# Moving the loop over overfull experts into the first expert pair, with a longer run of weight loads ahead of it

## The chip, the cores and the metric

The kernel runs on one core of one Trainium2 chip. The metric is the device time of one launch in microseconds; lower is better. The five instruction streams are TensorE (PE in the profile, with its weight loads shown as PEld), VectorE (DVE), ScalarE (ACT), GpSimd (POOL) and SyncE (SP). SP issues nearly all the weight transfers; the core's 16 DMA engines carry them out. All data are float32.

## The reference, cut to what matters

Three transformer layers run one after the other on 256 tokens of width 1024. Each layer first computes a modulation vector (silu of a condition vector times a weight matrix), then a mixer (attention, or in the third layer a mixture of attention, an MLP over chunks and a gated recurrence), and then a mixture of experts. The change touches the last part, which in the first two layers is:

```python
def grouped_moe(h, router_w, router_bias, w_gate, w_up, w_down):
    scores = sigmoid(t @ router_w)                 # 16 experts in 4 groups
    ...                                            # best group, then the best 2 of its 4 experts
    for e in range(N_EXPERTS):
        he = silu(t @ w_gate[e]) * (t @ w_up[e])   # 1024 -> 512
        out = out + gates[:, e:e + 1] * (he @ w_down[e])
```

The third layer has 32 experts and another router. An expert's three matrices are 2 MB each, so all experts together are 96, 96 and 192 MB, and every byte is read once.

## The kernel before, in words

**Experts in pairs.** `moe` handles two experts at a time, each with room for `CAP` = 64 tokens, so that the two fill 128 rows. `gather` (L1569) collects the tokens of eight experts with one-hot matrices. Then `body` runs for each pair: gate and up products (L1650), silu (L1655) and product (L1657), a transpose (L1666, copied on ACT in L1668), the down product (L1679), a weighting (`weigh`, L1684 to L1686), and one pair later `scatter` (L1714) back to the tokens, added to `x` (L1719). `back` (L1579) prepares the scatter matrix of a pair.

**Weight loads.** A pair needs 12 tiles of 1 MB (`load`, L1609): four each for gate, up and down. They live in the pool `u`, which has 17 such buffers, and SP issues them in program order. The loads are asked for by the letter `u` in an order string (each `u` is one step of the generator `ahead`), and at the head of each pair for those not yet asked for. Two more buffers of the pool hold the normalized tokens (`xs`) throughout the experts.

**The order strings.** `MIX_ORDER[0]`, `MIX_ORDER[1]` and `W2_ORDER` list, a letter at a time, the steps of the mixer of layers 0, 1 and 2 and the preparation of the experts: `M` the router's logits (two steps), `E` `ranks` (which expert and which place for each token, its products in L1527 to L1531), `F` the one-hot matrix of the first eight experts, `U` a broadcast of a modulation row (L443), `O` the gates, `L` a half of the gather, `l` `back`, `u` a load, `A` and `f` one modulation tile (`ada_tile`, two loads of 1 MB in L224 and eight products in L413), `9` a step of the third layer's context, interleaved into the second layer. A scheduler then orders each engine's instructions; SP's loads come out in the order of the strings, while the products of PE can move past one another unless `keep_in_program_order` pins them.

**The loop.** An expert may draw more than 64 tokens. `overflow` covers that with a hardware loop over such experts (L1728 reads their number `ni` into a register of each engine, L1729 is the loop). With this input the number is zero in all three layers; no line of the loop's body has an instruction in the trace. All five engines still meet at the loop's head and jump over its body. In the order strings the loop is the letter `!`, behind 12, 10 and 14 loads in layers 0, 1 and 2. What the program lists behind the loop can't be issued ahead of it, on any engine, SP among them. Once the strings are played, layer 0 and 1 close the next layer's modulation (`ada_close`: a copy of the sum, an add in L420 and 64 small products in L428), and `body` begins.

```python
        def ahead():
            for e0, n in ((0, 12), (2, 6)):
                for i in range(n):
                    load(e0, i)
                    yield
```

Of the kernel before, what the change touches and what calls it, by code (L numbers as in the profile page):

```python
# [11 lines left out]
F32R = mybir.dt.float32r  # L12
# [30 lines left out]
def _pack(inp):  # L43
# [68 lines left out]
    for l in range(3):  # L112
        bi = np.zeros((32, 512), np.float32)
        bi[:12] = (g("ada_b")[l] if l < 2 else g("b_mod_2")[0]).reshape(12, 512)
        if l == 2:
# [4 lines left out]

RAW = 2

W2_ORDER = "8f8GGKGKfKQQGfVVfKQfAYZZfQYb5QaBmanN6abc6bndW5cp4dc2mp43nfd2J.mqP13pq7r0sq107rHssTHXRergMijkMEFuOLULluuuuuuuuuuuuu!"
MIX_ORDER = ("00kkfkqiqvtfvqr4vf421321Kxw3xuzwzfKfyQKQyfVnTVQRAn55667JV78A8o.WPYXWXZYZfNpNeafbMdDuMEUFOLAuu,LuuuluuuuAu!uu",
             "0A0kkkqqqtvfvviffrKA12324341fKQxfKwxfyyQzzfQAIwTVR557667VJ.XV88oPYWWXYZ9Z9peabMdDUM9EFOLuLluuuuuuuuu!uuuu")
PRIME = 2

ENG = {
# [17 lines left out]
NB4 = 0  # L146

GE = 8
BUFS = {"u": 17, "b4": 8, "b2": 8, "tiny": 14, "G": 1}


class Halves:
# [10 lines left out]
class Gen:  # L163
# [223 lines left out]
                self.z2 = z  # L387
        return {"l": l, "lo": lo, "hi": hi, "n": 0}

    def ada_tile(self, st, V=None):  # L390

        n = st["n"]
        i = st["lo"] + n
        st["n"] += 1
        w = self.wload(self.ada_src(st["l"], i))
        if n == 0:
            st["R"] = self.ps()
        if i == max(st["lo"], st["hi"] - 3):
            b = f"bi{st['l']}"
            st["bi"] = self.late("b2", b, b, 32, self.nc.scalar)(b)  # L400
        z = self.z if st["l"] < 2 else self.z2
        last = i == st["hi"] - 1
        if V and n and not last:
            acc = self.t("b2", [128, 512])
            V.tensor_scalar(acc, w[:, 0, :], z[:, 0, 11:12], None, op0=OP.mult)
            for k in range(1, KC):
                V.scalar_tensor_tensor(acc, w[:, k, :], z[:, k, 11:12], acc, op0=OP.mult, op1=OP.add)
            self.nc.tensor.matmul(st["R"][0:32, :], self.unit[:, 11 - i:43 - i], acc, start=False, stop=False,
                                  skip_group_check=True)
            return  # L410
        for k in range(KC):
            j = k % 4
            self.nc.tensor.matmul(st["R"][32 * j:32 * j + 32, :], z[:, k, 11 - i:43 - i], w[:, k, :],  # L413
                                  start=(n == 0 and k < 4), stop=(last and k >= 4), skip_group_check=True)

    def ada_close(self, st):
        nc, l = self.nc, st["l"]
# [1065 lines left out]
    def moe(self, l, stG, side):  # L1483

        nc, tc, a = self.nc, self.tc, self.a
        V, A, G = nc.vector, nc.scalar, nc.gpsimd
        E = 16 if l < 2 else 32
# [5 lines left out]
        B_ = self.mod[l][:, 3]  # L1493
# [28 lines left out]
        def ranks():  # L1522

            mask = st["mask"] = self.t("tiny", [128, NT, E])
            st["rest"] = (self.route_a if l < 2 else self.route_b)(st["lg"], gates, mask)
            pr = st["pr"] = self.ps()
            nc.tensor.matmul(pr[:, 0:E], self.c("ut"), mask[:, 0], start=True, stop=True)  # L1527
            nc.tensor.matmul(pr[:, E:2 * E], self.c("ut"), mask[:, 1], start=True, stop=False)
            nc.tensor.matmul(pr[:, E:2 * E], self.ones, mask[:, 0], start=False, stop=True)
            for t in range(NT):  # L1530
                nc.tensor.matmul(pr[:, 128:128 + E], self.ones, mask[:, t], start=(t == 0), stop=(t == 1))  # L1531
            mf = mask.rearrange("p t e -> p (t e)")
            V.scalar_tensor_tensor(rk.rearrange("p t e -> p (t e)"), pr[:, :NT * E], -BIGR, mf, op0=OP.add, op1=OP.mult)
# [76 lines left out]
                W[(e0, *key)] = q  # L1610

        def ahead():
            for e0, n in ((0, 12), (2, 6)):
                for i in range(n):
                    load(e0, i)
                    yield

        def gathers():
            st["hs"] = rows_of()
# [6 lines left out]
        acts = {".": lambda: st.update(rw=self.late("b2", rn, rn)(rn)), "U": lambda: st.update(g2=self.bcast(stG(), 5, "G")), "E": ranks, "F": first, "O": gate_parts,  # L1626
                "l": lambda: st.update(nxt=back(st["Pt"], 0))}

        acts["!"] = lambda: self.overflow(l, E, st["xs"], A_, B_, gates, st["mask"], rk, ov, ni, st["g2"], wg, wu, wd)

        def body():
            g2, nxt = st["g2"], st["nxt"]
            hs, P = st["hs"], st["Pt"]
            pend = []
            for pr_ in range(E // 2):
                e0 = 2 * pr_
                for i in range(12):
                    load(e0, i)
                PT, gs = nxt
                more = pr_ + 1 < E // 2  # L1640
                turn = more and (e0 + 2) % GE == 0
                if turn:
                    P = places(e0 + 2)
                c0 = e0 % GE * CAP
                pgu = []
                for nm in "gu":
                    p = self.ps()
                    for k in range(KC):
                        for s in range(2):
                            nc.tensor.matmul(p[s * 64:(s + 1) * 64, :], hs[k // 2][:, k % 2, c0 + s * 64:c0 + (s + 1) * 64],  # L1650
                                             W[e0, nm, k // 4, s][:, k % 4, :], start=(k == 0), stop=(k == KC - 1), skip_group_check=True)
                    pgu.append(p)
                    if nm == "g":
                        sg = self.t("b2", [128, 512])
                        A.activation(sg, p, AF.Silu)  # L1655
                he = self.t("b2", [128, 512])
                V.tensor_mul(he, sg, pgu[1])  # L1657

                if pend:
                    self.scatter(pend, range(2))  # L1660
                if turn:
                    hs = rows_of()
                    gather(P, hs, 0)
                ph = self.ps()
                for k in range(4):
                    nc.tensor.transpose(ph[:, k * 128:(k + 1) * 128], he[:, k:512:4], self.ident)  # L1666
                heT = self.t("b2", [128, 4, 128])
                A.copy(heT, ph.rearrange("p (k c) -> p k c", k=4))  # L1668
                if turn:
                    gather(P, hs, 1)  # L1670
                if more:
                    nxt = back(P, e0 + 2)
                po = [self.ps() for _ in range(2)]
                oh, ol = (self.t("b4", [128, 2, 512], F32R) for _ in range(2))
                pend = [(PT, (oh, ol))]

                def down(n, k, w):
                    for s in range(2):
                        nc.tensor.matmul(po[n][s * 64:(s + 1) * 64, :], heT[:, k, s * 64:(s + 1) * 64], w(s),  # L1679
                                         start=(k == 0), stop=(k == 3), skip_group_check=True)  # L1680

                def weigh(n):
                    o = self.t("b2", [128, 512])
                    V.scalar_tensor_tensor(o, po[n], gs, g2[:, n * 512:(n + 1) * 512], op0=OP.mult, op1=OP.mult)  # L1684
                    A.copy(oh[:, n], o)  # L1685
                    (G if more else V).tensor_tensor(ol[:, n], o, oh[:, n].bitcast(F32), op=OP.subtract)  # L1686

                if more:
                    for h in range(2):
                        for n in range(2):  # L1690
                            for k in range(2 * h, 2 * h + 2):
                                down(n, k, lambda s: W[e0, "d", h, s][:, k % 2, n * 512:(n + 1) * 512])
                    next(side, None)
                    for n in range(2):
                        weigh(n)
                else:
                    for n in range(2):
                        for k in range(4):
                            down(n, k, lambda s: W[e0, "d", n, s][:, k])
                        weigh(n)  # L1700
                    for n in range(2):
                        self.scatter(pend, (n,), l == max(self.layers))
# [89 lines left out]
    def run(self):  # L1792
# [7 lines left out]
            st[key] = self.ada_open(l, lo, hi)  # L1800
            q[c].extend([st[key]] * (hi - lo))

        def fill(c, V=None):
            if q[c]:
                self.ada_tile(q[c].pop(0), V)

        def done(key):

# [10 lines left out]
        def layer(l, nxt):  # L1819
            self.l = l  # L1820
            ada(l, 4, 10, f"B{l}")
            ada(l, 10, 12, f"G{l}")
            if nxt:
                ada(l + 1, 0, 4, f"A{l + 1}", "A")
            steps, acts, body = self.moe(l, lambda: done(f"G{l}"), side)
            steps["9"] = side
            acts["f"] = lambda: fill("f")
            acts[","] = lambda: fill("f", self.nc.vector)
            if nxt:
                acts["A"] = lambda: fill("A")  # L1830
                acts["C"] = lambda: done(f"A{l + 1}")
            stB = lambda: done(f"B{l}")
            if l < 2:
                self.mix(l, stB, (steps, acts))
            else:
                self.mix2(stB, (steps, acts))
            if nxt:
                done(f"A{l + 1}")
            body()
# [52 lines left out]
```

## Time and profile before

| | |
|---|---|
| median of 3 runs | 1563.3 us (1558.73 to 1563.33) |
| the profiled execution | 1559.93 us, of which the span is 1558.1 us |
| moved by DMA | 540.85 MB, mean 347 GB/s |
| busy: PE / DVE / ACT / POOL | 1398.8 / 628.2 / 403.0 / 111.6 us |
| mean granted clock of TensorE | 0.966 of full speed |

The profile divides the span into busy time of each engine, the share of time that the DMA engines were busy, and the waits of each engine by what ended them. A busy share is a mean over the span: layer 0's mixer ends near 200 us and its experts near 440, layer 1's experts run from 644 to 885, and layer 2's from 1094 to the end. In the transfers a share near 1.0 at about 420 GB/s is the most that any stretch shows. The two levels of TensorE's clock appear as 1.00 and 0.50.

### The profile page before, as it was taken

Reading aid. Unit: us, or ns where it says so; the run is one execution under the profiler, and the core shown is the slowest. Engines: PE = TensorE matmul, PEld = TensorE weight load, DVE = VectorE, ACT = ScalarE, POOL = GpSimd, SP = SyncE. Lnnn points to the kernel's source line nnn. Section 1 sums busy time; section 2 is a strip of 40 time slices with the busy share of each in tenths; the row PEclk is TensorE's granted clock in tenths of the full one; section 3 lists DMA queues with packets and bytes.
Section 4 is the critical chain, followed back from the end, with each engine's and each line's share of the span. In section 5 each row is a group of like instructions: output and inputs, shape, how many; then the busy total and the mean of one; then the engine's idle time right before and its main releaser. Section 6 shows DMA issues by size and latency. Waiting matters only on the chain. (4 is left out here: it accounts for less than half of the span.)

```text
span 1558.1 us, 18392 instructions
## 1 busy us (share of the span) xinstructions
PE 1398.8 (90%) x7074; PEld 738.3 (47%) x7074; DVE 628.2 (40%) x1441; ACT 403.0 (26%) x717; POOL 111.6 (7%) x96
## 2 busy tenths in 40 slices
PE   5999889998879989899999898697899989988987
PEld 2676543443346556434544375475235434334332
DVE  3777621221176675243212569865022212212122
ACT  2455311011053553232111365532101011101000
POOL 0000101101000000001001000101001010001000
PEclk9999979999999999999999999798999999999999
DMA  9987859999989947499999967147899999999997
GB/s 363 330 328 275 342 201 422 421 421 421 413 309 380 349 162 308 180 415 415 421 421 420 356 219 273 60 136 297 322 421 421 421 421 421 421 421 421 420 422 294
DMA packets 131071, 540.85 MB, mean 347 GB/s; under 512 B 8600, under 2 KB 13856, under 8 KB 83360
## 3 DMA queue, kind: packets, MB, share of 16 engines
q1 hardware_dynamic: 128032, 533.73, 86.4%
q10 hardware_dynamic: 2320, 3.89, 0.8%
q0 software_dynamic: 624, 1.98, 0.4%
q8 instruction: 59, 0.97, 0.2%
q14 instruction: 36, 0.29, 0.1%
HBM read 538.49 MB, written 1.06 MB: 346 GB/s over the span
## 5 line engine op out<-in xcount | busy, mean ns | idle before, releaser
L1650 PE MATMUL ps<-u,b 128*64 128x512 f32 x2048 | 471.8, 600 | 49.2 <-DMA u<-in_w_dram 32.0
L1650 PEld LDWEIGHTS ps<-u,b 128*64 128x64 f32 x2048 | 160.6, 138 | 348.7 <-issue 264.8
L265 PE MATMUL ps<-u 128*128 128x512 f32 x1104 | 279.1, 403 | 6.9 <-ACT u L517 5.5
L1679 PE MATMUL ps<-u,b 128*64 128x512 f32 x1024 | 233.9, 597 | 13.7 <-ACT b L1668 13.7
L265 PEld LDWEIGHTS ps<-u 128*128 128x128 f32 x1104 | 203.5, 190 | 79.6 <-issue 23.0
L1657 DVE TENSOR_TENSOR b<-b,ps 128x512 f32<-128x512 f32 x32 | 22.0, 688 | 483.4 <-PE ps L1650 467.7
L1679 PEld LDWEIGHTS ps<-u,b 128*64 128x64 f32 x1024 | 78.1, 136 | 143.7 <-issue 122.9
L1686 POOL TENSOR_TENSOR b<-b,b 128x512 fp32r<-128x512 f32 x58 | 78.0, 1356 | 800.4 <-ACT b L1685 699.7
L1684 DVE SCALAR_TENSOR_TENSOR b<-ps,tiny,G 128x512 f32<-128x512 f32 x64 | 48.0, 750 | 179.8 <-PE ps L1679 177.7
L196 DVE TENSOR_TENSOR u<-u 128x2048 fp32r<-128x2048 f32 (+1 forms) x48 | 105.4, 2208 | 4.8 <-ACT u L185 4.7
L413 PE MATMUL ps<-u,z 128*32 128x512 f32 x576 | 83.5, 638 | 16.3 <-DVE z L382 13.2
L1685 ACT CAST b<-b 128x512 fp32r<-128x512 f32 x64 | 39.4, 618 | 206.3 <-DVE b L1684 206.3
L185 ACT CAST u<-u 128x2048 fp32r<-128x2048 f32 x44 | 82.7, 1913 | 17.8 <-DMA u<-in_a_w_qkv_dram 15.2
L1668 ACT COPY b<-ps 128x512 f32<-128x512 f32 x32 | 18.7, 585 | 259.7 <-PE ps L1666 259.7
L1719 DVE TENSOR_TENSOR x<-x,ps 128x512 f32<-128x512 f32 x128 | 79.4, 679 | 1.8 <-PE ps L1714 1.8
L1569 PE MATMUL ps<-b,u 128*128 128x512 f32 x256 | 72.2, 438 | 3.1 <-DVE b L1555 3.1
L1655 ACT ACTIVATE b<-ps 128x512 f32<-128x512 f32 x32 | 19.1, 597 | 210.7 <-PE ps L1650 210.7
L1714 PE MATMUL ps<-b,b 128*128 128x512 f32 x256 | 69.4, 409 | 3.2 <-DVE b L1686 1.9
L1569 PEld LDWEIGHTS ps<-b,u 128*128 128x128 f32 x256 | 66.2, 330 | 7.9 <-DVE b L1555 3.3
L1714 PEld LDWEIGHTS ps<-b,b 128*128 128x128 f32 x256 | 45.3, 188 | 39.4 <-issue 26.0
L185 ACT COPY b<-ps 128x512 f32<-128x512 f32 (+1 forms) x61 | 32.5, 558 | 72.6 <-PE ps L265 34.8
L517 ACT ACTIVATE b<-ps,mod,mA 128x512 f32<-128x512 f32 x32 | 24.9, 780 | 100.5 <-PE ps L1569 100.5
(346 smaller groups left out, 1125.5 us busy)
## 6 DMA issues: line engine op xcount, KB each, us to landing
u<-in_w_dram SPq DMA_DIRECT2D x192, 1024.0 KB, 19.8
u<-in_moe_w_gate_dram SPq DMA_DIRECT2D x64, 1024.0 KB, 14.4
u<-in_moe_w_up_dram SPq DMA_DIRECT2D x64, 1024.0 KB, 16.2
u<-in_moe_w_down_dram SPq DMA_DIRECT2D x64, 1024.0 KB, 16.8
u<-in_ada_w_dram SPq DMA_DIRECT2D x48, 1024.0 KB, 10.1
u<-in_w_mod_dram SPq DMA_DIRECT2D x24, 1024.0 KB, 7.2
u<-in_w_in_dram SPq DMA_DIRECT2D x14, 1024.0 KB, 7.3
u<-in_a_w_qkv_dram SPq DMA_DIRECT2D x12, 1024.0 KB, 14.6
```

The source lines that it names most:

```text
L185: (e.copy if e is self.nc.scalar else e.tensor_copy)(out, in_)
L196: self.pick(site, options).tensor_tensor(out, a, b, op=op)
L265: self.nc.tensor.matmul(p, x[a][:, k, t * 128:(t + 1) * 128], w[b][:, k % 4], start=start and i == 0 and k == ks[0], stop=stop and i == 2 ...
L413: self.nc.tensor.matmul(st["R"][32 * j:32 * j + 32, :], z[:, k, 11 - i:43 - i], w[:, k, :], start=(n == 0 and k < 4), stop=(last and k >= ...
L1569: nc.tensor.matmul(p, q[:, t, k:D:KC], P[:, t], start=(t == 0 and i == 0), stop=(t == 1 and i == 1))
L1650: nc.tensor.matmul(p[s * 64:(s + 1) * 64, :], hs[k // 2][:, k % 2, c0 + s * 64:c0 + (s + 1) * 64], W[e0, nm, k // 4, s][:, k % 4, :], star ...
L1679: nc.tensor.matmul(po[n][s * 64:(s + 1) * 64, :], heT[:, k, s * 64:(s + 1) * 64], w(s), start=(k == 0), stop=(k == 3), skip_group_check=True)
L1684: V.scalar_tensor_tensor(o, po[n], gs, g2[:, n * 512:(n + 1) * 512], op0=OP.mult, op1=OP.mult)
L1685: A.copy(oh[:, n], o)
L1686: (G if more else V).tensor_tensor(ol[:, n], o, oh[:, n].bitcast(F32), op=OP.subtract)
L1714: ins = nc.tensor.matmul(p, PT[:, t * 128:(t + 1) * 128], o[:, n, :], start=(i == 0), stop=(i == len(ops) - 1))
L1719: nc.vector.tensor_add(xs, xs, p)
```

## The change

The letter `!` leaves the order strings. The loop is now called inside `body`, in the first pair, between its down products and its weighting. `ahead` no longer lists 18 loads but 12 + `SECOND[l]`, that is 28, 24 and 28 in the three layers; those that the strings don't ask for are asked for at the head of the first pair, before its products. The strings ask for 17, 13 and 17 (before: 14 in each, those behind `!` included). The pool `u` gets an 18th buffer, and `b4` and `b2` a ninth. In layer 0 the two modulation tiles of the next layer that stood behind the gather (letters `A`) become two letters `=` ahead of `E`: their 16 products and the first product of `ranks` are pinned in this order. The output buffers of a pair (`oh`, `ol`) are taken later.

```diff
-W2_ORDER = "...MEFuOLULluuuuuuuuuuuuu!"
-MIX_ORDER = ("...DuMEUFOLAuu,LuuuluuuuAu!uu",
-             "...DUM9EFOLuLluuuuuuuuu!uuuu")
+W2_ORDER = "...MEFuOLULluuuuuuuuuuuuuuuu"
+MIX_ORDER = ("...DuM==EUFOLuu,Luuuluuuuuuuuuu",
+             "...DUM9EFOLuLluuuuuuuuuuuu")
-BUFS = {"u": 17, "b4": 8, "b2": 8, "tiny": 14, "G": 1}
+SECOND = (16, 12, 16)
+BUFS = {"u": 18, "b4": 9, "b2": 9, "tiny": 14, "G": 1}
...
-            self.nc.tensor.matmul(st["R"][32 * j:32 * j + 32, :], z[:, k, 11 - i:43 - i], w[:, k, :],
-                                  start=(n == 0 and k < 4), stop=(last and k >= 4), skip_group_check=True)
+            ins = self.nc.tensor.matmul(st["R"][32 * j:32 * j + 32, :], z[:, k, 11 - i:43 - i], w[:, k, :],
+                                        start=(n == 0 and k < 4), stop=(last and k >= 4), skip_group_check=True)
+            if pin:
+                self.tc.keep_in_program_order(ins)
...
-            nc.tensor.matmul(pr[:, 0:E], self.c("ut"), mask[:, 0], start=True, stop=True)
+            ins = nc.tensor.matmul(pr[:, 0:E], self.c("ut"), mask[:, 0], start=True, stop=True)
+            if l == 0:
+                tc.keep_in_program_order(ins)
...
-            for e0, n in ((0, 12), (2, 6)):
-                for i in range(n):
-                    load(e0, i)
-                    yield
+            for i in range(12 + SECOND[l]):
+                load(i // 12 * 2, i % 12)
+                yield
...
-        acts["!"] = lambda: self.overflow(l, E, st["xs"], A_, B_, gates, st["mask"], rk, ov, ni, st["g2"], wg, wu, wd)
+        over = lambda: self.overflow(l, E, st["xs"], A_, B_, gates, st["mask"], rk, ov, ni, st["g2"], wg, wu, wd)
...
                 for i in range(12):
                     load(e0, i)
+                for i in range(0 if pr_ else SECOND[l]):
+                    load(2 + i // 12 * 2, i % 12)
...
-                oh, ol = (self.t("b4", [128, 2, 512], F32R) for _ in range(2))
-                pend = [(PT, (oh, ol))]
...
+                    if not pr_:
+                        over()
+                    pend = [places_out()]
                     next(side, None)
                     for n in range(2):
                         weigh(n)
...
+                acts["="] = lambda: fill("A", pin=True)
```

## Rows read from the trace of the kernel before

**Rows 1.** Stretches: busy us of the engines, granted clock, DMA share, GB/s.
```profile
230.00:440.00 210.00, 194.94 (x881) 82.76 (x878) 43.23 (x75) 24.28 (x43) 18.73 (x14) 1.00 1.02 418
650.00:885.00 235.00, 223.46 (x1002) 102.77 (x999) 67.05 (x154) 49.22 (x79) 19.79 (x17) 0.99 1.02 415
885.00:1080.00 195.00, 166.65 (x1173) 114.14 (x1172) 149.80 (x360) 91.05 (x153) 11.60 (x11) 0.92 0.59 212
```

**Rows 2.** The same view, narrow, around the three loops.
```profile
162.00:201.00 39.00, 31.22 (x183) 21.42 (x182) 22.45 (x77) 9.37 (x18) 7.39 (x4) 0.84 1.00 398
201.00:217.00 16.00, 15.08 (x62) 10.02 (x60) 5.57 (x15) 5.12 (x8) 0.00 (x0) 0.85 0.02 6
226.50:228.50 2.00, 2.00 (x12) 0.67 (x10) 0.00 (x0) 0.00 (x0) 0.00 (x0) 1.00 0.42 107
...
624.80:645.00 20.20, 15.86 (x62) 12.20 (x62) 10.25 (x34) 5.32 (x9) 1.60 (x1) 0.92 0.02 6
...
1079.50:1092.00 12.50, 10.00 (x34) 8.18 (x32) 4.39 (x14) 4.78 (x8) 0.00 (x0) 0.86 0.03 10
...
1096.00:1102.00 6.00, 6.00 (x20) 1.74 (x18) 0.00 (x0) 0.00 (x0) 0.00 (x0) 0.67 0.06 14
```

**Rows 3.** SP's load issues around the loops of layers 0, 1 and 2.
```profile
185.23 1.19 SPq L224 DMA_DIRECT2D u<-in_ada_w_dram  x2
...
216.77 2.76 SPq L1609 DMA_DIRECT2D u<-in_moe_w_gate_dram  x3
...
610.42 37.98 SPq L1609 DMA_DIRECT2D u<-in_moe_w_down_dram  x4
...
L1609 SPq DMA_DIRECT2D u<-in_w_dram x3: 332/335/432, 1091.7 to 1101.3; - x3
```

**Rows 4.** The loop's branches on PE: ns min, median, max, all three layers.
```profile
L1729 PEldq COMPARE_BRANCH  x9: 70/182/3269, 214.9 to 1094.4; - x9
```

**Rows 5.** PE in order of time: start, us, group, idle before it.
```profile
198.32 0.61 PE L1527 MATMUL ps<-tiny,cst 128*128 128x16 f32 x2 [5.02 <-DVE tiny L1429]
...
203.25 5.57 PE L1569 MATMUL ps<-b,u 128*128 128x512 f32 x16
208.74 1.06 PE L413 MATMUL ps<-u,z 128*32 128x512 f32 x8
...
214.16 1.92 PE L413 MATMUL ps<-u,z 128*32 128x512 f32 x16
218.84 2.11 PE L428 MATMUL ps<-cst,b 128*64 128x12 f32 x32 [2.75 <-DVE b L420]
220.78 11.43 PE L1650 MATMUL ps<-u,b 128*64 128x512 f32 x40
...
644.39 13.96 PE L1650 MATMUL ps<-u,b 128*64 128x512 f32 x64 [2.12 <-DVEq L1729]
...
1094.60 16.59 PE L1650 MATMUL ps<-u,b 128*64 128x512 f32 x64 [5.10 <-issue]
```

**Rows 6.** What PE waited for: layers 0, 1, 2 (us, times, longest).
```profile
PE ps L1650 <- DMA u<-in_moe_w_up_dram: 6.6, 5, 1.4
PE ps L1650 <- DMA u<-in_moe_w_gate_dram: 2.6, 2, 1.3
...
PE ps L1650 <- DVEq L1729: 2.1, 1, 2.1
...
PE ps L1650 <- DMA u<-in_w_dram: 32.0, 26, 1.4
```

**Rows 7.** The chain that ended last, in layer 2: start, us, what.
```profile
1120.59 13.73 PE ps L1650 x64
1134.32 2.05 PE ps L1714 x8
...
1137.51 7.09 PE ps L1679 x32
...
1516.28 19.83 DMA u<-in_w_dram
```

**Rows 8.** DMA issues by tile: count, KB each, median us to landing.
```profile
b<-in_pack_dram POOLq DMA_DIRECT2D x2, 64.0 KB, 5.1
```

More of the change, by code (lines that the diff above doesn't have):

```diff
@@ L121 @@
 RAW = 2
-W2_ORDER = "8f8GGKGKfKQQGfVVfKQfAYZZfQYb5QaBmanN6abc6bndW5cp4dc2mp43nfd2J.mqP13pq7r0sq107rHssTHXRergMijkMEFuOLULluuuuuuuuuuuuu!"
-MIX_ORDER = ("00kkfkqiqvtfvqr4vf421321Kxw3xuzwzfKfyQKQyfVnTVQRAn55667JV78A8o.WPYXWXZYZfNpNeafbMdDuMEUFOLAuu,LuuuluuuuAu!uu",
-             "0A0kkkqqqtvfvviffrKA12324341fKQxfKwxfyyQzzfQAIwTVR557667VJ.XV88oPYWWXYZ9Z9peabMdDUM9EFOLuLluuuuuuuuu!uuuu")
+W2_ORDER = "8f8GGKGKfKQQGfVVfKQfAYZZfQYb5QaBmanN6abc6bndW5cp4dc2mp43nfd2J.mqP13pq7r0sq107rHssTHXRergMijkMEFuOLULluuuuuuuuuuuuuuuu"
+MIX_ORDER = ("00kkfkqiqvtfvqr4vf421321Kxw3xuzwzfKfyQKQyfVnTVQRAn55667JV78A8o.WPYXWXZYZfNpNeafbMdDuM==EUFOLuu,Luuuluuuuuuuuuu",
+             "0A0kkkqqqtvfvviffrKA12324341fKQxfKwxfyyQzzfQAIwTVR557667VJ.XV88oPYWWXYZ9Z9peabMdDUM9EFOLuLluuuuuuuuuuuu")
 PRIME = 2
@@ L388, in ada_open, with ada_tile @@
         return {"l": l, "lo": lo, "hi": hi, "n": 0}
-    def ada_tile(self, st, V=None):
+    def ada_tile(self, st, V=None, pin=False):
         n = st["n"]
@@ L1680, in down, with places_out @@
                                          start=(k == 0), stop=(k == 3), skip_group_check=True)
+                def places_out():
+                    oh, ol = (self.t("b4", [128, 2, 512], F32R) for _ in range(2))
+                    return PT, (oh, ol)
                 def weigh(n):
+                    oh, ol = pend[0][1]
                     o = self.t("b2", [128, 512])
@@ L1696, in body @@
                 else:
+                    pend = [places_out()]
                     for n in range(2):
@@ L1801, in ada, with fill @@
             q[c].extend([st[key]] * (hi - lo))
-        def fill(c, V=None):
+        def fill(c, V=None, pin=False):
             if q[c]:
-                self.ada_tile(q[c].pop(0), V)
+                self.ada_tile(q[c].pop(0), V, pin)
         def done(key):
```

## The prediction

> **What bounds the kernel now.** I began with the stretches of the whole span [rows 1]. In the experts of layers 0 and 1 the transfers run at 415 to 418 GB/s with a DMA share of 1.02, so nothing more fits in; PE is busy for 93 and 95% there as well. In layer 2's mixer the share is 0.59, and its 28.3 us of idle PE are spread over short dependent steps. Next I asked which wait is last in each set of experts [rows 6]. In layer 0 PE waits for weights for 6.6 + 2.6 = 9.2 us in all, in layer 1 never (the row shown is its wait at the loop), in layer 2 for 32.0 us. So layer 2 is bound by transfers, layer 1 by PE, layer 0 by both within 9.2 us.
>
> Then the places where the transfers stand still, in narrow stretches [rows 2]. They rest at a share of 0.02 to 0.03 from 201 to 217, from 624.8 to 645 and from 1079.5 to 1092 us, each time at a loop. Two reasons meet there. SP sits at the head of the loop until the slowest engine has come, and behind it stand the next loads: it issues at 216.77, 644 and 1091.7 again [rows 3]. And the pool is nearly full: in layers 0 and 2 the transfers starve a second time after three loads and one (0.42 from 226.5 to 228.5, 0.06 from 1096 to 1102), until the first gate products give buffers back. In a set of experts bound by transfers such a hole is lost for good.
>
> **Prices.** One load is 1.05 MB at 418 GB/s, 2.5 us; a load lands 19.83 us after its issue [rows 7], so eight are in flight. A pair's gate and up products take 13.73 us, its down products 7.09, and 3.2 us lie between (1134.33 to 1137.51) [rows 7]. The first two buffers come free after a quarter of the 13.73 us, 3.4 us. From SP's issue to flowing data I count 1 us (issue at 1101.3, share near 1 from 1102) [rows 2, 3].
>
> **Layer 0: holes and start.** Before, 12 loads were done by 201 us, three followed at 216.77, and load 16 began at 228.5. After, 18 buffers less the two of the tokens hold 16 loads, provided that the modulation tiles have given theirs back. They have: pinned ahead of `ranks`, they fall into the 5.02 us for which PE waits for the routing anyway (ended at 198.32) [rows 5]. One and a half tiles are left for that gap, 1.06 + 1.92 = 3.0 us at full clock; at half clock 6.0, which would hold `ranks` up by 1 us. Their two loads per tile move forward on SP past pair 0's loads and are back in time: the last tile's were issued at 185.23 [rows 3] and now stand some eleven loads earlier. So the transfers go on for four loads, to 201 + 10 = 211 us.
>
> PE's order to pair 0 loses 1.06 us of a tile between the gathers, 1.92 us of one behind them, the loop's 2.75 us, and has 2.11 us of closing products that can go into a gap [rows 5]: `back` ended at 214.2, now near 213.1, and pair 0 starts between 213 and 216; I take 214.5 for 220.78, 6.3 us earlier. Load 17 flows at 214.5 + 3.4 + 1 = 218.9, which puts load 16 at 216.4 instead of 228.5: **12 us earlier** (10.6 to 13.6 by the start). Is PE fast enough? It gains 6.3 us, and 2.85 us because the first 40 products ran 11.43 us where 13.73 x 40 / 64 = 8.6 would do [rows 5, 7]; it loses the loop inside the pair (3 us, below). With its 9.2 us of waits that makes 15.4, so the 12 stand. With the dearest loop, a half-clock start and a start at 216 it makes 9.
>
> **The loop in its new place.** The register reads, the meeting and the jump are the same; the PE idle ahead of its next work was 2.75, 2.12 and 5.10 us [rows 5], the longest with a jump of 3.27 us [rows 4]. The trace shows no loop in mid-pair. Two things differ: ACT and DVE have nothing left that PE waits for, and SP comes after PE, since the last loads of the 28 (24) go out only as the down products free their buffers. I take 3 us, near the two shorter ones, and keep 2.1 to 5.1. After the 5.10 us the granted clock was 0.67 [rows 2] and the pair took 16.59 us for 13.73: 2.9 us more, which belongs to the dear end. Behind the loop now stand, on DVE, ACT and POOL, pair 0's weighting; who waits for it is the scatter, which comes after pair 1's 13.73 us, so nothing. On SP stand loads 29 and later. In layer 2, taking pair 0's start from the next paragraph, the down products end at 1089.5 + 13.7 + 3.2 + 7.1 = 1113.5; loads 17 to 28 flow from 1093.9 to 1123.9; the next buffers are free at 1113.5 + 3 + 3.4 and their loads flow at 1120.9: covered by 3 us. At the dear end (5.1 us, half clock) they flow at 1126.5, a hole of 2.6 us. Layer 0 has the same margin.
>
> **Layer 2.** 14 loads were done by 1079.5, one more followed, load 16 began at 1102. After: 16 loads without a pause to 1084.5; pair 0 starts where `back` ended, at 1094.60 - 5.10 = 1089.5; load 17 flows at 1089.5 + 3.4 + 1 = 1093.9, load 16 so to say at 1091.4: **10.6 us earlier**, 8 with the hole. PE follows, with 32 us of waits in hand.
>
> **Layer 1.** The same count would let the transfers resume about 5 us earlier, but PE never waits for them here, so this buys nothing. PE saves 2.1 us ahead of pair 0 and pays 3 behind its down products: **0.9 us slower**, between 2.1 faster (loop hidden altogether) and 5.9 slower (5.1 + 2.9 - 2.1).
>
> **Rest.** The ninth buffers of `b4` and `b2`, the later `oh` and `ol`, and the pins themselves issue nothing. They and the 18th buffer give the scheduler another order in the mixers, on either side; of the 28.3 us of idle PE in layer 2's mixer I allow a seventh, 4 us, each way.
>
> **Sum.** 12 - 0.9 + 10.6 = 21.7 us off the profiled execution's 1559.9: 1538. That execution lies 3.4 us under the median of the runs, so I forecast **1540 us**.
>
> **A rule that speaks against it.** In the rows, one jump of PE cost 3.27 us and the median of the nine 0.18 [rows 4]. The Trainium skill (Runtime: NRT & Kernel Launch, section "Instruction fetch mechanics") says that a taken branch whose target lies outside the two pages at hand makes the engine wait for a DMA fetch. By that rule every skip of a long loop body would pay, and the first rival below would hold; the trace bears it out for one loop in three.
>
> **Rivals.** *Dear loop:* all three loops stall PE for 5.1 us and the clock falls to its half each time. With a stall of S us (above 3) the gains become 14.6 - S in layer 0, -0.8 - S in layer 1 and 13.2 - S in layer 2, together 27 - 3S; at 5.1 that is 11.7, or 1548 us. *Slower:* the same mechanism, but the fetch queues behind the weights, which now run at full share while the loops before found the DMA idle (0.02 to 0.03) [rows 2]. The formula passes zero at S = 9 us and 0.3% slower at 10.6. If the fetch landed as late as a load does, 19.8 us, the sum is 32 us slower, 1592. Against it: 64 KB pieces on another queue land after 5.1 us [rows 8] while the loads' own queue takes 19.8. *The lead does not come:* some tile keeps two buffers through the gathers, 14 loads stand ready instead of 16, and the change moves little but the loop. Layers 0 and 2 lose two loads each, 5 us: 21.7 - 10 = 11.7, or 1548. The full pool of before (12 loads, 2 of the tokens and 3 loads more make 17 in layer 0) speaks against it. *The mixers:* the new order costs what the experts gain, 15 to 20 us, in stretches where PE has 0.59 of DMA share beside it [rows 1]: about 1560.
>
> **Chances.** The forecast, 1530 to 1547: 0.55. Dear loop: 0.15. No lead: 0.08. Mixers eat it: 0.08. Slower by the fetch: 0.09. Better than 1530 because the extra buffers help the mixers too: 0.05. What a measurement can tell from no change is about 0.3%, 4.7 us. Faster than that: 0.55 + 0.15 + 0.08 + 0.05, less 0.02 for tails, 0.81; within 0.3%: the mixers' 0.08 and a little of the tails, 0.09; slower: 0.10. The range 1530 to 1556 leaves out the slower case, most of the mixers' case and the best one, 0.2 in all.
>
> **What would show it.** Right: no hole in the transfers from 162 to 211 us, then one hole of 8 us (211 to 219) where there were two, and in layer 2 one of some 9 us where there were 12.5 and 6; load 16 near 216 in layer 0, near 1080 in layer 2 by its own clock (1091 less layer 0's 12, plus 1); PE's waits for weights in layer 0 down from 9.2 to about 3 us (15.4 - 12). Layer 1's experts as long as before within 2 us. At each loop, now between L1679 of pair 0 and L1650 of pair 1, 2 to 5 us of idle PE with a DMA share still near 1. Wrong: an idle PE of over 9 us there, a DMA share that falls behind the loop, `ranks` of layer 0 later than 199 us, or mixers that are longer than before.

## The result, and the profile after

The changed kernel takes **1577.45 us** (median of 4 runs, 1575.23 to 1578.81), the kernel before 1562.99 us beside it: a ratio of 1.0107, 95% interval 1.0092 to 1.0122. It is 1% slower, where 1540 us was forecast. The profiled execution took 1578.81 us, its span 1577.0, 18.9 us more than the span before.

What PE waited for answers to [rows 6]; the line of gate and up products is now L1659, the loop is L1745, the mixer's line that stands behind the loop in layer 1 is L529:

```profile
PE ps L1659 <- SPq L1745: 30.5, 2, 15.5
PE ps L1659 <- DMA u<-in_w_dram: 26.2, 22, 1.3
...
PE ps L529 <- SPq L1745: 14.5, 1, 14.5
...
PE ps L1659 <- DMA u<-in_moe_w_up_dram: 2.6, 2, 1.3
PE ps L1659 <- DMA u<-in_moe_w_gate_dram: 0.6, 1, 0.6
```

Waits for weights went down, in layer 0 from 9.2 to 3.2 us, as far as forecast. But PE now stands 45 us at the loop, 15 in each layer, and what releases it is SP. In order of time (start, us, group, idle before it), around the starts of [rows 5] and around the loop's new place:

```profile
191.36 5.72 PE L416 MATMUL ps<-u,z 128*32 128x512 f32 x32
198.33 0.40 PE L1532 MATMUL ps<-tiny,cst 128*128 128x16 f32 x2 [1.25 <-DVE tiny L1434]
...
213.89 16.70 PE L1659 MATMUL ps<-u,b 128*64 128x512 f32 x64
...
232.91 7.09 PE L1686 MATMUL ps<-u,b 128*64 128x512 f32 x32 [0.49 <-ACT b L1677]
254.91 7.67 PE L1659 MATMUL ps<-u,b 128*64 128x512 f32 x22 [14.92 <-SPq L1745]
...
661.29 7.14 PE L1686 MATMUL ps<-u,b 128*64 128x512 f32 x32 [0.49 <-ACT b L1677]
682.97 9.18 PE L529 MATMUL ps<-u 128*128 128x512 f32 x16 [14.54 <-SPq L1745]
...
1122.91 7.14 PE L1686 MATMUL ps<-u,b 128*64 128x512 f32 x32 [0.47 <-ACT b L1677]
1145.58 16.79 PE L1659 MATMUL ps<-u,b 128*64 128x512 f32 x64 [15.53 <-SPq L1745]
```

The down products of pair 0 (L1686) end at 240.0, 668.4 and 1130.1 us; then PE does nothing until 254.9, 683.0 and 1145.6. The stretches around the first two show what the transfers did meanwhile (us of PE, PEld, DVE, ACT and POOL, granted clock, DMA share, GB/s):

```profile
240.00:250.00 10.00, 0.00 (x0) 0.00 (x0) 0.00 (x0) 0.00 (x0) 0.00 (x0) 0.67 1.02 422
251.00:252.00 1.00, 0.00 (x0) 0.00 (x0) 0.00 (x0) 0.00 (x0) 0.00 (x0) 0.50 0.69 287
252.00:253.00 1.00, 0.00 (x0) 0.00 (x0) 0.00 (x0) 0.00 (x0) 0.00 (x0) 0.50 0.12 49
253.00:254.00 1.00, 0.00 (x0) 0.00 (x0) 0.00 (x0) 0.00 (x0) 0.00 (x0) 0.50 0.02 8
254.00:262.00 8.00, 7.09 (x22) 2.15 (x24) 1.41 (x2) 1.24 (x2) 2.49 (x2) 0.60 0.00 2
262.00:264.00 2.00, 2.00 (x12) 0.69 (x10) 0.00 (x0) 0.00 (x0) 0.00 (x0) 1.00 0.87 221
...
682.00:692.00 10.00, 9.03 (x16) 3.75 (x16) 1.41 (x2) 0.00 (x0) 0.00 (x0) 0.74 0.00 1
```

Read them from the top: the weights flow at full rate while PE and every other engine do nothing; at 252 us they run out; at 254.9 us PE starts again; and only then, in a pool full of weights, does PE free the buffers for the next loads, which flow at 262. One stall thus opened a hole of 10 us in the transfers. In the hole's first part the granted clock is 0.50 to 0.60, near or at the lower of TensorE's two levels (1.2 of 2.4 GHz), behind 15 us without a product. Layer 2's pair 1 (its row at 1145.58) took 16.79 us where a pair at the full clock takes 13.95.

That PE starts when the last load has landed is no coincidence. The loop's semaphore events step through the stall; in each row: engine, kind, count, ns, first and last start:

```profile
L1745 SPq EVENT_SEMAPHORE  x2: 17/17/17, 246.5 to 249.0; - x2
L1745 ACTq EVENT_SEMAPHORE  x2: 38/38/38, 246.5 to 249.0; - x2
L1745 PEldq EVENT_SEMAPHORE  x2: 51/51/51, 246.5 to 249.0; - x2
...
L1745 SPq EVENT_SEMAPHORE  x1: 17/17/17, 251.5 to 251.5; - x1
L1745 PEldq EVENT_SEMAPHORE  x1: 51/51/51, 251.5 to 251.5; - x1
...
L1745 SPq EVENT_SEMAPHORE  x5: 17/17/17, 253.9 to 254.2; - x5
L1745 PEldq EVENT_SEMAPHORE  x6: 51/51/51, 253.9 to 254.5; - x6
```

At 246.5, 249.0 and 251.5 the engines get past one semaphore each, at 253.9 past the rest, all at the same moments, 2.5 us apart: that is the 2.5 us of one load. The program itself names what they wait for. In its list of instructions, SP's way past the body of layer 0's loop is a wait for `SP_sequencer_49`, then one wait each for `DMAHW0_49` to `DMAHW7_49`, then an unconditional branch. These eight are the semaphores on which SP's loads report, and the counts asked for are those of all 84 transfers issued on them up to there. At the loop's end each of the five engines, PE among them, waits for the same eight once more, and for the counters of the others. So my **theory after the result**: no engine passes this loop, though it turns no time, until every transfer in flight has landed. The loads that were to cover the loop are what it waits for. The **rival** is the one of the prediction: the jump over the loop's code is fetched behind the weights. Both would show a stall that ends near the end of the transfers.

### The profile page after: what moved, and what is told of

Its sections match the earlier page's. It is cut to its first block, busy times and chain, and to the rows that moved or that the text cites. A ratio compares the mean times of both kernels' runs of the same rounds, so it can differ in the third digit from the quotient of the medians.

```text
span 1577.0 us, 18361 instructions
## 1 busy us (share of the span) xinstructions
PE 1395.4 (88%) x7074; PEld 741.7 (47%) x7074; DVE 628.2 (40%) x1441; ACT 402.8 (26%) x717; POOL 109.6 (7%) x96
## 5 line engine op out<-in xcount | busy, mean ns | idle before, releaser
L1659 PE MATMUL ps<-u,b 128*64 128x512 f32 x2048 | 467.0, 603 | 60.3 <-SPq L1745 30.5
L1659 PEld LDWEIGHTS ps<-u,b 128*64 128x64 f32 x2048 | 161.9, 139 | 354.9 <-issue 296.3
L1686 PE MATMUL ps<-u,b 128*64 128x512 f32 x1024 | 231.2, 596 | 13.6 <-ACT b L1677 13.6
L1686 PEld LDWEIGHTS ps<-u,b 128*64 128x64 f32 x1024 | 77.8, 137 | 142.6 <-issue 121.5
L187 ACT CAST u<-u 128x2048 fp32r<-128x2048 f32 x44 | 82.6, 1908 | 15.3 <-DMA u<-in_a_w_qkv_dram 15.3
## 6 DMA issues: line engine op xcount, KB each, us to landing
u<-in_moe_w_down_dram SPq DMA_DIRECT2D x64, 1024.0 KB, 15.3
```

The source lines that it names most:

```text
L187: (e.copy if e is self.nc.scalar else e.tensor_copy)(out, in_)
```

## The experiments

Each run is compared with the kernel before on the same chip; its medians there were 1560.5 to 1561.4 us. For all of them, this table gives how long each layer took in the profiled execution, from the end of the last scatter of one layer's experts to the next (layer 0 from the span's start), in us. The end is read off the mixer's first product, less its wait: for the changed kernel 446.62 less 4.35. Executions of one kernel differ by some microseconds (the kernel before: spans of 1555.4 to 1561.4 us on one chip), and a row is one execution, so a difference of a microsecond or two in a layer decides nothing.

| kernel | layer 0 | layer 1 | layer 2 | span | median |
|---|---|---|---|---|---|
| before | 440.6 | 439.3 | 678.2 | 1558.1 | 1560.5 to 1563.0 |
| changed | 442.3 | 452.7 | 682.1 | 1577.0 | 1577.45 |
| changed, no loop (e1) | 430.6 | 439.7 | 670.5 | 1540.8 | 1543.40 |
| before, no loop (e7) | 440.6 | 437.8 | 669.3 | 1547.7 | 1550.12 |
| no loop, no pins (e10) | 435.4 | 439.0 | 671.0 | 1545.4 | 1548.72 |
| no loop, old buffers (e11) | 435.7 | 438.9 | 669.1 | 1543.7 | 1547.41 |
| lead 4, 0, 4 (e4) | 453.4 | 454.4 | 690.1 | 1597.9 | 1599.69 |
| lead 12, 8, 12 (e2) | 438.0 | 441.7 | 675.7 | 1555.4 | 1558.19 |
| lead 14, 10, 14 (e12) | 439.5 | 449.3 | 675.3 | 1564.1 | 1565.90 |
| short loop (e8_short_loop) | 442.2 | 451.1 | 679.6 | 1572.9 | 1575.02 |
| loop's loads by POOL (e8_pool_in_loop) | 442.3 | 451.5 | 679.5 | 1573.3 | 1576.65 |
| loop in its old place (e3) | 434.2 | 437.0 | 676.0 | 1547.3 | 1548.39 |
| layer 2's loop last (e9) | 434.7 | 437.0 | 670.9 | 1542.7 | 1543.91 |
| the same, pools of 8 (e13) | 432.3 | 438.5 | 674.7 | 1545.5 | 1549.03 |

**What the loop costs, new place and old.** First the changed kernel without it:

```diff
-                    if not pr_:
-                        over()
```

> The changed kernel without the loop over overfull experts: it leaves out the meeting of the engines and the jump, nothing that this input needs. Theory (the loop's head waits until every transfer that SP has issued has landed, so the lead can't cover it): the 14.5 to 15.5 us of idle PE behind pair 0's down products are gone in all three layers, the transfers run on without a pause behind load 17, and the lead is worth what it was forecast to be: layer 0's experts end near 429 us (442 in the changed kernel), in all about 25 us under the kernel before, 1536 to 1543 us. Rival (the loss comes from the other edits: three larger pools, pinned tiles, another order in the mixers): the time stays above 1555 us.

Measured: 1543.40 us, ratio 0.9895 (0.9873 to 0.9917). The whole loss is the loop: 36.2 us of span, 11.7, 12.9 and 11.6 in the three layers. The rest of the change gains 17.3 us of span, where about 25 had been expected of it, and the time lies just above the expected range. The same edit in the kernel before:

```diff
-...uuuuuuuuuuuuu!"     -...uuuuAu!uu"     -...uuuuuuuuu!uuuu"
+...uuuuuuuuuuuuu"      +...uuuuAuuu"      +...uuuuuuuuuuuuu"
```

> The kernel before with the loop over experts with too many tokens left out (with these inputs it turns no time). PE stands 2.8, 2.1 and 5.1 us ahead of pair 0 for it, and SP's loads pause for it: 1549 to 1556 us if these stalls lie on the path. If the weights set the time whatever stands ahead of pair 0 (17 buffers, so no more loads can be ahead): 1558 to 1563 us. What the version without the loop gains over this one is what buffers, lead and the two pinned tiles are worth by themselves.

Measured: 1550.12 us, ratio 0.9937 (0.9919 to 0.9955). In its old place the loop had cost 10.4 us of span, nothing in layer 0, 1.5 in layer 1 and 8.9 in layer 2. (Layer 0's nothing hides something: `ranks` began at 200.68 us for 198.32, so its mixer took 2.4 us longer here and the rest of the layer as much less.) Between this kernel and the one above lie buffers, lead and pins, 6.9 us of span: 10.0 gained in layer 0, 2.7 of them ahead of `ranks`, and 3.1 lost in layers 1 and 2.

**How the stall goes with the lead.** If the loop waits for what is in flight, fewer loads ahead of it must shorten the stall, one load by one load's time.

```diff
-SECOND = (16, 12, 16)
+SECOND = (12, 8, 12)       # then (4, 0, 4), then (14, 10, 14)
```

> The changed kernel with 24, 20 and 24 loads ahead of the loop instead of 28, 24 and 28. Theory (wait for landing): the 24th load lands about when the down products end, so nothing is left to wait for; PE idles 2 to 5 us at the loop instead of 15, the transfers pause some 5 us instead of 10, and the time falls to 1546 to 1555 us: a shorter lead is faster. Rivals: if the idle time comes from the jump's code that is fetched behind the weights, or from the meeting in mid-pair as such, PE idles 12 to 15 us as before and the time stays at 1575 to 1580.

Measured: 1558.19 us, ratio 0.9986 (0.9975 to 0.9997). Stalls of 4.7, 5.9 and 4.5 us, about as expected (2 to 5); the time came out a little above. Against the changed kernel the stalls are 30 us shorter in all and the span only 21.6. The whole loop had shown the same: 45 us of stall cost 36.2 of span.

> The changed kernel with the loop inside pair 0, but only 16, 12 and 16 loads ahead of it, so that SP reaches the loop early and every transfer has landed long before PE comes. Theory (wait for landing): PE idles 2 to 5 us at the loop; the price moves to the transfers, which pause from about 211 to 244 us in layer 0 and alike in the others, so that PE waits for weights afterwards; time 1575 to 1595 us. Rivals (code fetch behind weights would be quick here too, 2 to 5 us; the meeting in mid-pair as such: 15 us).

Measured: 1599.69 us (one run). The stalls fell to 1.8, 5.3 and 2.1 us, about as expected; when PE came to layer 1's loop, at 677.6 us, nothing was in flight (a DMA share of 0.00 from 672 to 678), so its 5.3 are not a wait for loads. But the kernel is the slowest of all, 5 us beyond what was expected. With four loads of the second pair ahead SP sits at the loop, with nothing more to issue, until PE has come, and the transfers stand still (stretches as above, layer 0):

```profile
225.00:232.00 7.00, 7.00 (x36) 2.24 (x32) 0.00 (x0) 0.60 (x1) 0.00 (x0) 1.00 0.00 0
232.00:240.00 8.00, 6.65 (x36) 2.61 (x34) 1.01 (x3) 0.86 (x2) 0.00 (x0) 1.00 0.00 0
240.00:244.00 4.00, 2.23 (x12) 0.57 (x10) 1.41 (x2) 0.97 (x2) 0.31 (x1) 1.00 0.22 43
```

So both ends of the lead are dear: few loads ahead leave the transfers idle ahead of the loop, many make the loop wait. Then a point in between:

> The changed kernel with 14, 10 and 14 loads of the second pair and beyond ahead of the loop, in place of 16, 12 and 16. Theory (the loop waits until the transfers in flight have landed, 2.5 us for each load): the stalls lie midway between 15 us and the 5 us that 12, 8 and 12 gave, 9 to 11 us each, 1564 to 1572 us. Rival (a fixed price of a branch that misses, paid once there is enough traffic): 13 to 16 us each, 1572 to 1580 us.

Measured: 1565.90 us (one run), and all three stalls fall in the theory's 9 to 11 us (PE in order of time):

```profile
252.09 15.53 PE L1659 MATMUL ps<-u,b 128*64 128x512 f32 x64 [10.14 <-SPq L1745]
...
675.92 10.13 PE L529 MATMUL ps<-u 128*128 128x512 f32 x16 [10.06 <-SPq L1745]
...
1131.23 16.28 PE L1659 MATMUL ps<-u,b 128*64 128x512 f32 x64 [9.53 <-SPq L1745]
```

12, 14 and 16 loads (8, 10 and 12 in layer 1) give 5, 10 and 15 us: 2.5 us for a load, without a step. This fits a wait for landing. A fetch that queues behind the weights could follow the same line, so the next two runs separate them.

**Code length, or transfers?** The loop's body cut to a few instructions, with its loads still on all eight of SP's semaphores:

```diff
+            for i in range(8):
+                t = wts[i % 2]
+                nc.sync.dma_start(t, wg[bass.ds(ev, 1)]...)
+                nc.tensor.matmul(p[:, 0:128], self.ident, t[:, 0, 0:128], start=(i == 0), stop=(i == 7))
-            ...                # the body's other lines
```

> The changed kernel with the loop's body cut down to eight weight quarters, each read by one small matmul (the rest of the work for an expert with too many tokens is left out; with these inputs the loop turns no time). The loop's code becomes short, so a branch across it goes a short way; its transfers still use all eight of SP's semaphore lanes, so that SP's branch at the loop's head still waits for all of them. Theory (the head waits until SP's transfers have landed): the three stalls stay at 13 to 16 us, transfers pause for 9 to 11 us each time, 1570 to 1580 us. Rival (the long jump's code is fetched behind the weights): the stalls fall to 0 to 4 us, 1542 to 1552 us.

Measured: 1575.02 us (1574.39 to 1577.16), ratio 1.01 (1.008 to 1.0119), with the stall unmoved (PE in order of time, layer 0):

```profile
255.26 6.99 PE L1659 MATMUL ps<-u,b 128*64 128x512 f32 x22 [14.73 <-SPq L1745]
```

In layers 1 and 2 PE stood 14.2 and 14.9 us. PE's branches at the loop (ns min, median, max), in the changed kernel and here:

```profile
L1745 PEldq COMPARE_BRANCH  x9: 70/196/6101, 236.2 to 1145.2; - x9
L1745 PEldq COMPARE_BRANCH  x9: 70/178/305, 236.8 to 1141.1; - x9
```

The rival falls: with no branch over 0.3 us PE waits as long. The 2.4 us that it is faster lie within the two kernels' scatter. Then the other half: the body as long as ever, its loads issued by POOL, so that SP's branch no longer names any load.

```diff
-                nc.sync.dma_start(t, src[:, kq * 2:kq * 2 + 2, n0:n0 + 512])
+                nc.gpsimd.dma_start(t, src[:, kq * 2:kq * 2 + 2, n0:n0 + 512])
-            ev = nc.values_load(ei[0:1, 0:1], engines=[SP], min_val=0, max_val=E - 1)
+            ev = nc.values_load(ei[0:1, 0:1], engines=[POOL], min_val=0, max_val=E - 1)
```

> The changed kernel, whole, with the loop's own weight quarters issued by POOL in place of SP: the loop is as long as before and stands at the same place behind the same loads, but SP's branch at its head waits for none of SP's lanes, and the lanes that POOL's branch waits for have long been idle. Theory (the head waits until SP's transfers have landed): the stalls fall to 1 to 5 us each, no pause of the transfers, 1544 to 1555 us (1541 without the loop and three stalls of 1 to 5 us). Rival (the long jump's code is fetched behind the weights): stalls stay at 13 to 16 us, 1570 to 1580 us. Second rival (the join behind the loop waits for every lane whoever issued): as the first rival in time, with the PE waiting for SP at the loop's line.

Measured: 1576.65 us (1573.13 to 1578.13), ratio 1.0105 (1.008 to 1.0129). The first theory's number did not come; the second rival did. SP's way past the body names no semaphore now, and still PE stands (first fence, PE in order of time) and every engine steps with the loads (second fence, the loop's semaphore events):

```profile
255.77 6.41 PE L1659 MATMUL ps<-u,b 128*64 128x512 f32 x20 [14.97 <-DMA u<-in_moe_w_gate_dram]
```
```profile
L1745 SPq EVENT_SEMAPHORE  x1: 28/28/28, 252.4 to 252.4; - x1
L1745 ACTq EVENT_SEMAPHORE  x1: 38/38/38, 252.4 to 252.4; - x1
L1745 POOLq EVENT_SEMAPHORE  x1: 43/43/43, 252.4 to 252.4; - x1
L1745 DVEq EVENT_SEMAPHORE  x1: 50/50/50, 252.4 to 252.4; - x1
L1745 PEldq EVENT_SEMAPHORE  x1: 51/51/51, 252.4 to 252.4; - x1
```

Layers 1 and 2 stood 14.0 and 15.4 us. So the wait is not SP's alone, and not for the semaphores that the loop itself uses. In this kernel's list of instructions the end of the loop names them all, the eight of SP's queue, those of POOL's and every engine's own, on each of the five engines. The theory stands in a wider form: the loop, as this program builds it, is a fence for the loads in flight, whatever its body is and whoever issues the body's own loads. In every run the loads in flight were SP's; that it would hold up POOL's transfers too is read from the list alone.

**Places that have nothing in flight.** Lead, buffers and pins of the change, and the loop back ahead of pair 0, behind 16, 12 and 16 loads:

```diff
+        acts["!"] = lambda: self.overflow(l, E, ...)
-"...FOLuu,Luuuluuuuuuuuuu"    -"...FOLuLluuuuuuuuuuuu"    -"...FuOLULluuuuuuuuuuuuuuuu"
+"...FOLuu,Luuuluuuuuuuuu!u"   +"...FOLuLluuuuuuuuuuu!u"   +"...FuOLULluuuuuuuuuuuuuuu!u"
```

> The changed kernel with its pools, pins and strings, but with the loop back at the end of the strings, behind 16, 12 and 16 loads (all that the pool holds) and ahead of pair 0. Theory: those loads land while PE still gathers (near 211, 630 and 1085 us by the clock of the kernel before, the gathers end at 209, 642 and 1089), so the loop costs PE the 2 to 5 us that it cost before and no more; layers 0 and 2 keep a part of the gain, layer 1 stays as it was: 1546 to 1554 us. Rival (the other edits lose): 1560 us or more.

Measured: 1548.39 us, ratio 0.9924 (0.9902 to 0.9947), faster than both kernels. When PE reaches the loop the transfers have stopped already (a DMA share of 0.01 from 625 to 638 us, 0.02 from 1078 to 1087), so PE stands only for the meeting and the jump: 2.2 us ahead of pair 0 in layer 1, 5.5 in layer 2. Layer 2 is 5.5 us longer than without a loop. There the loop can stand at the very end, where no load is left:

```diff
+                    if l == 2:
+                        acts["!"]()        # last pair: behind its down products, ahead of its scatter
```

> The version with the loop in its old place behind 16, 12 and 16 loads ahead, but layer 2's loop moved behind the last pair's down products, where no transfer is left to wait for. Layer 2 from the end of layer 1's experts takes 4.5 us more there than without a loop at all, of which the loop's end of the chain can give back at most that and takes the barrier and PE's jump: 1543 to 1549 us. Rival (the jump on the last chain costs PE 5 us or more, as the old one did): 1549 to 1553 us.

Measured: **1543.91 us**, ratio 0.9895 (0.9877 to 0.9913): 17 us under the kernel before on that chip (1560.96), and level with the version that has no loop at all (1543.40; layer 0 is 4.1 us longer, layer 1 2.7 shorter). The last pair in order of time, here (first fence) and without the loop:

```profile
1518.23 3.65 PE L1659 MATMUL ps<-u,b 128*64 128x512 f32 x14 [1.33 <-SPq L1745]
1521.81 2.11 PE L1730 MATMUL ps<-b,b 128*128 128x512 f32 x8
1523.76 0.63 PE L1675 MATMUL ps<-IG,b 128*128 128x128 f32 x4
1525.07 7.43 PE L1686 MATMUL ps<-u,b 128*64 128x512 f32 x32 [0.68 <-ACT b L1677]
1534.61 1.76 PE L1730 MATMUL ps<-b,b 128*128 128x512 f32 x5 [2.11 <-ACT b L1697]
```
```profile
1525.49 7.45 PE L1686 MATMUL ps<-u,b 128*64 128x512 f32 x32 [0.68 <-ACT b L1677]
1532.87 1.21 PE L1728 MATMUL ps<-b,b 128*128 128x512 f32 x4
1534.44 0.49 PE L1728 MATMUL ps<-b,b 128*128 128x512 f32 x1 [0.35 <-ACT b L1697]
```

Without the loop the last scatter begins as the down products end; with it PE idles 2.11 us there. From the start of the down products to the end of the span it is 17.6 us with the loop (1542.7 less 1525.07) and 15.3 without (1540.8 less 1525.49): here the loop costs 2.3 us. That layer 2 as a whole is only 0.4 us longer (670.9) is due to a mixer that took 2.1 us less.

**Which part gains in layer 0.** Both runs leave the loop out and take one part back:

```diff
-"...DuM==EUFOLuu,Luuuluuuuuuuuuu"          # first run: no pinned tiles
+"...DuMEUFOLAuu,LuuuluuuuAuuuuuu"
-BUFS = {"u": 18, "b4": 9, "b2": 9, ...}     # second run: the old pools
+BUFS = {"u": 17, "b4": 8, "b2": 8, ...}
```

> The version without the loop, and without the two pinned modulation tiles: they stand again where the kernel before has them, among the loads of layer 0, and the ranks' first matmul is free (the loop is left out; with these inputs it turns no time). Theory (the earlier start of layer 0's pair 0 is what lets the loads go on, since all buffers are full by then): pair 0 at 219 to 222 us, layer 0's experts end 5 to 9 us later, 1548 to 1553 us. Rival (the buffers and the loads ahead bring layer 0's gain by themselves): pair 0 may be late, layer 0's experts end within 2 us of the version with the pins, 1541 to 1546 us.

> The version without the loop, with 17, 8 and 8 buffers as in the kernel before, in place of 18, 9 and 9 (the loop is left out; with these inputs it turns no time). One load of 2.5 us fewer stands ahead at each layer's pair 0. Theory (each buffer is worth its load where the transfers set the time): layers 0 and 2 lose 2.5 us each, 1545 to 1550 us. Rival (the 7 us that the mixers of layers 1 and 2 take longer than in the kernel before without its loop come with the buffers): these come back, 1538 to 1543 us.

Measured: 1548.72 us, ratio 0.9923 (0.9906 to 0.994), with pair 0 at 219.1 us and layer 0 longer by 4.8; and 1547.41 us, ratio 0.9913 (0.9896 to 0.9929), with layer 0 longer by 5.2. So the pins bring about half of layer 0's 10 us. Of the 5.2 us that the old pools cost there, 2.5 lie in the mixer (`ranks` at 200.48 us for 197.99); the other 2.7 are about one load, as the theory had it. In layer 2 the old pools gave back 4.2 us in the mixer, the rival's part (207.6 us from the end of layer 1 to pair 0, for 211.8), and lost 2.8 in the experts, one load again. That suggested one more version, weights' pool at 18 and the small ones at 8:

> The version with layer 2's loop behind the last pair's down products, with 18, 8 and 8 buffers in place of 18, 9 and 9. With 17, 8 and 8 buffers and no loop, layer 2's mixer took 207.6 us in place of 211.8. Theory (the mixer's loss comes with the ninth buffers of the two small pools, the experts' gain with the eighteenth weight buffer): layer 2's mixer 1 to 3 us shorter than in the version with 9 and 9, the experts as there, 1539 to 1543 us. Rival (the loss comes with the eighteenth weight buffer, through the transfers beside the mixer): the mixer as with 9 and 9, 1543 to 1546 us.

Measured: 1549.03 us (1547.05 to 1549.61), ratio 0.9922 (0.9909 to 0.9936). A miss: layer 2's mixer became 3.4 us longer, not shorter (213.1 us for 209.7). What sets the mixers' time from one version to the next stays open; no row here ties it to one pool.

## Why the prediction was wrong, step by step

**The step that failed** is the loop in its new place: the term "I take 3 us", which measured 15.0 in each layer, and the words "covered by 3 us". The count of loads was right, loads 17 to 28 were indeed in flight behind the down products; they were taken for cover, and they are what the loop waits for. A loop of 3 us became one of 15, and the loads behind it, reckoned at 1120.9 us in layer 2, ahead of the end of the transfers, left a hole of 10, 13 and 11 us in the three layers (layer 0's from 252 to 262 above). The prediction's own sign for this, idle PE of over 9 us and a DMA share that falls behind the loop, is what came.

**The formula came near by luck.** For a stall of S us it gave a gain of 27 - 3S. With the 15.0 us measured (45 / 3) that is 18 us slower, 1578 us for the profiled execution, which took 1578.8. But the runs split it otherwise: without the loop the span gains 17.3 us, not 27, and the loop takes 36.2, not 45. The first was 9.7 us too large and the second 8.8, and the errors cancel. The rival that carried the formula beyond its zero had 0.09, with a fetch behind the weights as the reason; the short loop shows that the reason was another. The row on which the 3 us rested [rows 5] had the wait in it, hidden: in the kernel before the loop waits for the same semaphores, but the DMA share had been 0.02 to 0.03 for 10 us and more by then [rows 2], so nothing was left to wait for. I read that as the price of the loop; it was the price of a loop with nothing in flight. The place that answers "what does this wait for" was the loop's list of semaphores, not its duration.

**The jump.** Long jumps did come, 6.1 us for one PE branch of the changed kernel. It began at 668.7 us in layer 1, just behind pair 0's down products, and was over at 674.8, when the loop's semaphores still held PE until 682.6. The short loop, whose longest PE branch took 0.3 us, stood as long, so a long jump is not the price that this change paid. The Trainium skill's rule (Runtime: NRT & Kernel Launch, section "Instruction fetch mechanics"), that a taken branch out of the pages at hand waits for a fetch, fits the 6.1 us, in one loop of three.

**What came as forecast.** In layer 0 `ranks` began at 198.33 (198.32 before), the two pinned tiles fill the gap, and pair 0 started at 213.9 us (214.5 forecast). Without the loop layer 0 gains 10.0 us; forecast were 12. The missing 2 are the second half of the hole, which ends at 221 us in that run and not at 219, because pair 0 began at the lower clock (0.57 from 211 to 219 us).

**Right by accident.** PE's waits for weights in layer 0 fell to the 3.2 us that were forecast, but the lead did not do that: without the loop they are 7.9 us (5.3 for up, 2.6 for gate), and with leads of 12 and 14 in front of the loop 6.2 and 3.9. PE's long stand at the loop let the loads get ahead of it.

**Layer 1** was forecast 0.9 us slower, with 3 us of it the loop's, so 2.1 us faster without one. Without the loop it is 0.4 slower; its mixer took 1.0 us longer. The loop's 12.9 came on top.

**Layer 2.** Forecast were 10.6 us. Where the loop is gone the experts bear that out; pair 0 in the kernel before without its loop, and in the change without it:

```profile
1085.75 13.95 PE L1650 MATMUL ps<-u,b 128*64 128x512 f32 x64
1082.09 13.95 PE L1659 MATMUL ps<-u,b 128*64 128x512 f32 x64
```

From there to the end of the span it is 462.0 and 458.7 us. In the kernel before it was 468.6 from the end of `back` (1089.5). So 9.9 us came in the experts, 6.6 of them because the loop no longer stands ahead of pair 0 and 3.3 with the larger pools and the longer lead; with the longer lead and the old pools it is 461.5, so 2.8 of the 3.3 came with the pools. The mixer took 2.1 us longer, which leaves the layer's 7.7. The kernel before without its loop gains more in the whole layer, 8.9, only because its mixer took 4.4 us less than that of the change (207.3 for 211.8).

**The mixers** were allowed 4 us each way. With the loop they took 1.0 us (layer 1) and 2.1 us (layer 2) longer than before, counted to the end of `back`; that is within the allowance, on the bad side, and not explained. Without the loop they were as long (202.7 and 211.8 us, for 201.7 and 209.6 before), so it is not the loop that lengthened them.

## What to carry to other kernels

The loop of this kernel, with a count that is read at run time, is a fence even if it turns no time: everything in flight must land first, and PE restarts at the lower clock. The waits are instructions that the program carries around the loop; a loop built without them was not tried. Put such a loop where the transfers have stopped anyway, or behind the last of them; a lead of loads hides many stalls, but never one that waits for loads. And when work in flight is to cover a wait, first look whether that work is in the list of what the wait names.

## What the runs showed of the hardware

The price of the program's fence is linear in what is in flight: 2.5 us for each 1 MB load (5, 10 and 15 us with 12, 14 and 16 loads). In layer 0 the last semaphore came at 253.9 us, some 2 us after the DMA share had fallen, and PE restarted 1 us later. A stall of 15 us cost about 12 us of span; behind it the granted clock was 0.50, and a pair's gate and up products took 16.8 us in layer 2 for 13.95. How the 12 us divide between this and the hole of 10 to 13 us in the transfers, no run separates. At the end of the program, behind the last transfer, the same loop cost 2.3 us.
